# Third of three fused blocks: convolution stages woven into other attention pairs, norm and pointwise product moved to the third pair

## The chip, the core and the metric

The kernel runs on one core of one Trainium2 chip. The metric is the device time of one execution in microseconds. All three blocks are one program; only the order of the third block is changed, together with one engine choice and one buffer count.

## The reference, cut to what matters

S = 1024 rows, D = 1024 channels, f32. Two earlier blocks hand x to the third:

```python
def third_block(x, ln_g, w_in, b_in, dw_w, dw_b, cln_g, cln_b, pw_w, pw_b, rpb,
              gn_conv_g, gn_att_g, w_out, final_g):
...
        hn = rms_norm(h, ln_g[l])
        proj = hn @ w_in[l] + b_in[l]
        glu_a, glu_b, z_conv, q, k, v, z_att = jnp.split(proj, cuts, axis=-1)
        y_conv = conformer_conv(glu_a, glu_b, dw_w[l], dw_b[l], cln_g[l], cln_b[l],
                                pw_w[l], pw_b[l])
        y_att = neighbourhood_attention(q, k, v, rpb[l])
        y_conv = grouped_rms_norm(y_conv, gn_conv_g[l], CONV_GROUPS) * jax.nn.silu(z_conv)
        y_att = grouped_rms_norm(y_att, gn_att_g[l], N_HEADS) * jax.nn.silu(z_att)
        y = jnp.concatenate([y_conv, y_att], axis=-1)
        h = h + y @ w_out[l]
    return rms_norm(h, final_g)
```

`conformer_conv` is u = a * sigmoid(b), a depthwise convolution of 31 taps along the rows, a layer norm over 512 channels, silu, and a product with a 512 x 512 matrix. `neighbourhood_attention` has 8 heads of 64 channels; each position sees a window of the 16 x 64 grid.

## The kernel before

All arrays that products read are kept feature-major: 128 channels on the partitions, positions along the free axis, in two halves of 512 positions. A product in f32 is made of three matmuls per 128 channels (`mm3`, L95, L96, L97): high x high, high x low, low x high, each 128x128 by 128x512. `weight()` loads one 128x1024 piece of a matrix by SP's queue, casts the high part (on DVE, L86, or on ACT, L84, when the list `hi_on` holds True) and makes the low part on POOL (L87). A product of one weight over one half of x is 24 matmuls.

Each engine executes its instructions in the order in which the program was scheduled; the order in which the code is written is its input. A PSUM tile that collects a product comes from the group "mm" (two buffers) or "mf" (one buffer), chosen by `lane`. Scores have their own "sp" (two), transposes "tr" (two), attention's output "pv" (one).

Block 3 is built of generators. `glu(i)` makes channels i*128.. of u from two weights (ACT tanh, DVE L1290, L1291). `dwconv(i, u)` is 31 instructions on DVE over 128x1024 (L1302 once, L1304 thirty times) and stores the result to DRAM (cv_d). `conv_ln(hf)` takes four tiles of 128 positions: load, four transposes (L1315), norm statistics, `xn` (L784), four transposes back (L1320), scale and bias and tanh on ACT, and the split into `cn` high and low. `conv_pw(hf)` multiplies `cn` with two weights, 48 matmuls, into v, and runs a gate after each weight. `zgate(i)` is one product of w_in with x, stored to DRAM (z_d). `na_pair(hp)`, called p0 to p3 here, handles two heads: 144 matmuls of projections q, k and v, the gate of the pair before, a yield, then eight attention steps (4 per head; scores L323, L324 into sp, transposes L346, products L359 into pv, the sum to `aT` L366). `group_norm_gate` is a gate: squares, a matmul that sums them (L1251 into "mf"), a copy to `gr` (L1252), Ln and Exp on ACT, two products on DVE (L1259, L1260), one on POOL, and the store to y_d; its z and gr have one buffer each. `known()` is the output product over the first six of eight channel pieces, 288 matmuls (tiles y3a), `w_out` the step in it. After the gate of p3 come the last 96 matmuls and the final norm.

`weave(main, *streams)` advances the streams by a share of their yields after each attention step of main; a number behind a generator is its count of yields, the last number of a stream is the number of steps over which it is spread.

In the order before, convolutions 0 and 1 run beside the first products and p0's projections, 2 and 3 in p0's attention; the norm and pointwise product of half 0 are in p1, of half 1 in p2, with zgates beside them; `known()` is in p3.

Of the kernel before, what the change touches and what calls it, by code (L numbers as in the profile page):

```python
# [10 lines left out]
F32 = mybir.dt.float32  # L11
# [7 lines left out]
P = 128  # L19
S = 1024  # L20
# [11 lines left out]
def kernel(ctx: ExitStack, tc: tile.TileContext, a, out, blocks=(1, 2, 3)):  # L32
    nc = tc.nc
    mm = nc.tensor.matmul
# [13 lines left out]
    def f(ap):  # L48
        return ap.bitcast(F32)
# [49 lines left out]
    lane, turn = ["any"], [0]  # L99
# [92 lines left out]
    def weave(main, *streams):  # L192


        left = [[st[0], [g for g, _ in st[1]], 0, sum(c for _, c in st[1]) / st[2]] for st in streams]

        def steps(st, upto):
            while st[1] and (upto is None or st[2] < upto):
                with on(st[0]):
                    if next(st[1][0], None) is None:  # L200
                        st[1].pop(0)
                    else:
                        st[2] += 1

        for i, _ in enumerate(main):
            for st in left:
                steps(st, st[3] * (i + 1))
        for st in left:
            steps(st, None)
# [50 lines left out]
    def heads_k(dst, dlo, src, hf, bias=None, view=same, dup=False):  # L260
        for h in range(2):
            o = 64 * h
            b = None if bias is None else bias[o:o + 64]
            hi, sv = view(dst[o:o + 64, h], src[o:o + 64], hf)
            if b is None:
                act(out=hi, in_=sv, func=AF.Copy)
            else:
                act(out=hi, in_=sv, func=AF.Identity, bias=b)
            other = view(dst[64 - o:128 - o, h], src[o:o + 64], hf)[0]
            if dup:  # L270
                nc.scalar.copy(other, hi)
            else:
                nc.gpsimd.tensor_copy(other, hi)
            for q in range(2) if dup else (h,):
                d, _ = view(dlo[64 * q:64 * q + 64, h] if len(dlo.shape) == 3 else dlo[o:o + 64], src[o:o + 64], hf)
                if b is None:
                    tt(out=d, in0=sv, in1=f(hi), op=ALU.subtract)
                else:
                    stt(out=d, in0=sv, scalar=b, in1=f(hi), op0=ALU.add, op1=ALU.subtract)  # L279
# [988 lines left out]
    def block3(x3, begin, finish):  # L1268
        x_st, x_fm = x3
        w3 = a["w_in_3"]  # L1270
        TAP, PAD = 31, 15
# [4 lines left out]
        np_ = pool("na", side="right", c=nas)  # L1276
# [3 lines left out]
        cp = pool("conv", side="right", c=us)  # L1280

        def glu(i):
            wb, wa = weight(w3[4 + i]), weight(w3[i])
            u = cp.tile([P, S + 2 * PAD], F32, name="u", tag="u", bufs=2)
            nc.gpsimd.memset(u[:, 0:PAD], 0.0)
            nc.gpsimd.memset(u[:, S + PAD:], 0.0)
            for hf in range(2):
                sg = cp.tile([P, HS], F32, name="sg", tag="sg", bufs=1)
                act(out=sg, in_=fm(wb, x_fm[hf]), func=AF.Tanh, scale=0.5, bias=col("b_in_3", 4 + i, half))
                ts(out=sg, in0=sg, scalar1=1.0, scalar2=0.5, op0=ALU.add, op1=ALU.mult)  # L1290
                stt(out=u[:, PAD + hf * HS:PAD + (hf + 1) * HS], in0=fm(wa, x_fm[hf]), scalar=col("b_in_3", i), in1=sg,  # L1291
                    op0=ALU.add, op1=ALU.mult)
                yield 1
            return u

        def dwconv(i, u):
            y = cp.tile([P, S], F32, name="cy", tag="cy", bufs=2)
            for k in range(TAP):
                w = col("dw_w_3", 4 * k + i)
                src = u[:, k:k + S]  # L1300
                if k == 0:
                    ts(out=y, in0=src, scalar1=w, scalar2=col("dw_b_3", i), op0=ALU.mult, op1=ALU.add)  # L1302
                else:
                    stt(out=y, in0=src, scalar=w, in1=y, op0=ALU.mult, op1=ALU.add)  # L1304
            nc.sync.dma_start(cv_d[i], y)

        def conv_ln(cp2, n_fm, hf):
# [42 lines left out]
        def zgate(pl, i):  # L1350
            j = 8 + i if i < 4 else 20 + i
            wz = weight(w3[j])
            for hf in range(2):
                zr = pl.tile([P, HS], F32, name="zr", tag="zr", bufs=2)
                act(out=zr, in_=fm(wz, x_fm[hf]), func=AF.Identity, bias=col("b_in_3", j))
                nc.sync.dma_start(z_d[i, :, hf * HS:(hf + 1) * HS], zr)
                yield 1
# [3 lines left out]
        def na_pair(hp):  # L1361
            wq, wk, wv = (weight(w3[j * 4 + hp]) for j in (3, 4, 5))
            qs = np_.tile([P, 2, S], F32R, name="qs", tag="qs", bufs=1)
            ks = np_.tile([P, 2, S], F32R, name="ks", tag="ks", bufs=1)
            kl = np_.tile([P, S], F32R, name="kl", tag="kl", bufs=1)
            vs = np_.tile([P, 2, NT, P], F32R, name="vs", tag="vs", bufs=1)
            vt = np_.tile([P, S], F32, name="vt", tag="pth", bufs=1)
            for hf in range(2):
                heads_q(qs, fm(wq, x_fm[hf]), hf, col("b_in_3", 12 + hp), to_grid_rev)
            for hf in range(2):  # L1370
                heads_k(ks, kl, fm(wk, x_fm[hf]), hf, col("b_in_3", 16 + hp), to_grid)
            if pend:
                for _ in na_gate(*pend.pop()):
                    pass
            for hf in range(2):
                d, sv = to_grid(vt, fm(wv, x_fm[hf]), hf)
                act(out=d, in_=sv, func=AF.Identity, bias=col("b_in_3", 20 + hp))
            heads_v(vs, vt)
            yield "in"
            aT = np_.tile([P, S], F32, name="aT", tag="vt", bufs=1)  # L1380
            for h in range(2):
                hd = 2 * hp + h
                hk = np_.tile([P, 384], F32, name="hk", tag="hk", bufs=1)
                nc.scalar.dma_start(hk, bass.AP(tensor=rpb_d.tensor, offset=rpb_d.offset + hd * 496,
                                                ap=[[16, 8], [8 * 496, 16], [1, 384]]))
                bias = np_.tile([P, 768], F32, name="bias", tag="bias", bufs=1)
                for j in range(2):
                    sl = slice(384 * j, 384 * (j + 1))
                    stt(out=bias[:, sl], in0=hk, scalar=8.0, in1=mask[:, sl], op0=ALU.mult, op1=ALU.add)

                def bias_of(t):
                    o = 0 if t in (0, NT - 1) else 384
                    return bias[:, o + (P if t == 0 else 0):o + (256 if t == NT - 1 else 384)]

                def dst_of(u, src, aT=aT, h=h):
                    o = aT[64 * h:64 * h + 64].rearrange("p (r c) -> p c r", c=64)[:, 16 * u:16 * u + 16]
                    return o, src.rearrange("p (c r) -> p c r", r=16)

                yield from attend_steps(np_, qs[:, h], qs[64 * h:64 * h + 64, h], ks[:, h], kl[64 * h:64 * h + 64], vs[:, h],
                                        bias_of, lambda t: (max(0, t - 1), min(NT, t + 2)), dst_of, smax=384, rev=True)  # L1400
            pend.append((hp, aT))
# [7 lines left out]
                for hf in range(2):  # L1409
                    split(last[hf][0][:, 0], last[hf][1][:, 0], r[:, hf])  # L1410

        def conv_in(i):
            u = yield from glu(i)
            dwconv(i, u)

        convs = [conv_in(i) for i in range(2)]
        lane[0] = "any"
        for c_ in convs:
            next(c_)
        lane[0] = "mf"  # L1420
        for c_ in convs:
            for _ in c_:
                pass
        lane[0] = "mm"
        hi_on[0] = True
        p0 = na_pair(0)
        next(p0)
        weave(p0, ("mf", [(conv_in(2), 2), (conv_in(3), 2), (zgate(np_, 4), 2)], 7))
        us.close()
        hi_on[0] = False  # L1430
        with ExitStack() as c:
            cp2 = pool("conv2", side="right", c=c)
            n_fm = [[], []]
            p1 = na_pair(1)
            next(p1)
            weave(p1, ("mf", [(conv_ln(cp2, n_fm[0], 0), 4)], 4),
                  ("mm", [(zgate(np_, i), 2) for i in (5, 0, 1, 2, 3)] + [(conv_pw(cp2, n_fm[0], 0), 6)], 8))
            p2 = na_pair(2)
            next(p2)
            weave(p2, ("mf", [(conv_ln(cp2, n_fm[1], 1), 4)], 4),  # L1440
                  ("mm", [(zgate(np_, i), 2) for i in (6, 7)] + [(conv_pw(cp2, n_fm[1], 1), 6)], 8))
            p3 = na_pair(3)
            next(p3)
        x_st.close()

        with ExitStack() as c:
# [27 lines left out]
            g = np_.tile([P, D], F32, name="fg", tag="qs", bufs=1)  # L1474
# [143 lines left out]
```

## Time and profile before

| | |
|---|---|
| time, median of 3 runs | 3422.62 us (3420.29 to 3425.85) |
| time of the profiled execution | 3422.53 us |
| its span | 3420.8 us |
| granted PE clock, mean | 0.975 |
| PE busy | 3239.9 us, 14976 matmuls |
| DVE busy | 2073.7 us |
| POOL busy | 1383.7 us |
| ACT busy | 1059.6 us |
| block 3, within the span | about 2786 to 3421 us |

The span is the time from the first to the last instruction of the profile; 1.7 us lie around it. PE's busy share is that of matmuls in flight, and a matmul at a lower granted clock counts longer. The shares are means over blocks that run quite differently, so a stage is read from its own stretch.

### The profile page before, as it was taken

What the parts mean: (1) busy time and instruction counts of PE and PEld (TensorE: products, weight loads), DVE (VectorE), ACT (ScalarE), POOL (GpSimd) and SP (SyncE); (2) the same over time, 40 slices, a digit from 0 to 9 for tenths busy, and PEclk for the clock granted to TensorE, in tenths of its full rate; (3) what the DMA queues carried; (4) which work ended last, traced back from release to release, by engine and by line L of the source; (5) the groups of instructions that cost most, each with busy time, mean ns of one, the idle gap of its engine ahead of it and who ended that gap; (6) DMA issues with size and microseconds to landing.
All of it is one profiled execution on the core that took longest, in us unless ns stands there. A gap on an engine that the chain in (4) does not pass through costs nothing. (4 is left out here: it accounts for less than half of the span.)

```text
span 3420.8 us, 39879 instructions
## 1 busy us (share of the span) xinstructions
PE 3239.9 (95%) x14976; PEld 2655.8 (78%) x14976; DVE 2073.7 (61%) x3256; ACT 1059.6 (31%) x1998; POOL 1383.7 (40%) x913
## 2 busy tenths in 40 slices
PE   7999999999999999999978999999999988998998
PEld 6888887877888788778867777788888866776776
DVE  5455556375444455557768866545445579995665
ACT  3333311032333310321235632332231132235552
POOL 3111131266555643233434367655564362132221
PEclk9999999999999999999999999999999998998899
DMA  4211124212222422222252121222243221122241
GB/s 139 69 58 57 60 71 164 77 47 71 78 84 83 152 97 63 92 72 90 87 187 62 38 74 59 74 84 83 84 148 99 80 89 38 59 84 83 79 148 68
DMA packets 107473, 293.33 MB, mean 86 GB/s; under 512 B 15232, under 2 KB 20608, under 8 KB 107280
## 3 DMA queue, kind: packets, MB, share of 16 engines
q1 hardware_dynamic: 79184, 240.75, 21.3%
q10 hardware_dynamic: 28096, 50.04, 4.3%
q8 instruction: 118, 1.93, 0.2%
q14 instruction: 75, 0.61, 0.1%
HBM read 227.24 MB, written 63.76 MB: 85 GB/s over the span
## 5 line engine op out<-in xcount | busy, mean ns | idle before, releaser
L87 POOL TENSOR_TENSOR w_lo<-w_raw,w_hi 128x1024 fp32r<-128x1024 f32 x187 | 470.3, 2520 | 1130.6 <-DVE w_hi L86 653.5
L95 PE MATMUL mm<-x,w_hi 128*128 128x512 f32 x688 | 276.5, 402 | 13.0 <-DVE kl L279 8.0
L96 PE MATMUL mm<-x,w_hi 128*128 128x512 f32 x688 | 273.9, 398 | 0.0
L97 PE MATMUL mm<-x,w_lo 128*128 128x512 f32 x688 | 272.5, 397 | 1.1 <-POOL w_lo L87 1.1
L438 POOL TENSOR_TENSOR w_lo<-s,w_hi 128x512 fp32r<-128x512 f32 x160 | 220.7, 1387 | 104.4 <-ACT w_hi L437 104.0
L95 PE MATMUL mf<-x,w_hi 128*128 128x512 f32 x576 | 232.0, 403 | 4.6 <-DVE u L1291 1.6
L97 PE MATMUL mf<-x,w_lo 128*128 128x512 f32 x576 | 228.2, 396 | 1.2 <-POOL w_lo L87 1.2
L96 PE MATMUL mf<-x,w_hi 128*128 128x512 f32 x576 | 229.0, 398 | 0.0
L565 DVE TENSOR_TENSOR h<-h,mm 128x512 f32<-128x512 f32 x214 | 146.6, 686 | 134.7 <-PE mm L97 134.6
L86 DVE CAST w_hi<-w_raw 128x1024 fp32r<-128x1024 f32 x143 | 135.6, 949 | 128.5 <-PE mm L96 55.6
L438 POOL TENSOR_TENSOR w_lo<-w_raw,w_hi 128x512 fp32r<-128x512 f32 x120 | 171.6, 1430 | 96.8 <-ACT w_hi L437 96.6
L1304 DVE SCALAR_TENSOR_TENSOR cy<-u,cols,cy 128x1024 f32<-128x1024 f32 x120 | 180.6, 1524 | 0.9
L519 DVE TENSOR_TENSOR u<-p,pb 128x512 f32<-128x512 f32 x40 | 27.5, 687 | 249.1 <-PE pb L97 249.1
L437 ACT CAST w_hi<-s 128x512 fp32r<-128x512 f32 x160 | 97.2, 619 | 243.6 <-PE pc L96 148.2
L95 PEld LDWEIGHTS mm<-x,w_hi 128*128 128x128 f32 x688 | 130.5, 190 | 44.4 <-issue 12.1
L335 ACT ACTIVATE st<-st,nmax 128x128 f32<-128x128 f32 (+5 forms) x192 | 119.3, 623 | 116.0 <-DVE nmax L329 110.1
L95 PE MATMUL mm<-w_hi,act 128*128 128x512 f32 x384 | 150.5, 392 | 2.9 <-DVE h L565 2.9
L97 PEld LDWEIGHTS mm<-x,w_lo 128*128 128x128 f32 x688 | 130.4, 189 | 29.4 <-POOL w_lo L87 1.7
L96 PEld LDWEIGHTS mm<-x,w_hi 128*128 128x128 f32 x688 | 130.6, 190 | 26.1 <-issue 1.6
L96 PE MATMUL mm<-w_lo,act 128*128 128x512 f32 x384 | 150.5, 392 | 0.3 <-POOL w_lo L87 0.3
L97 PE MATMUL mm<-w_hi,act 128*128 128x512 f32 x384 | 150.3, 392 | 0.0
L137 ACT ACTIVATE pth<-tr 128x512 fp32r<-128x512 f32 (+3 forms) x224 | 95.8, 451 | 148.6 <-PE tr L346 108.2
(502 smaller groups left out, 8876.4 us busy)
## 6 DMA issues: line engine op xcount, KB each, us to landing
w_raw<-in_w_ffn_in_dram SPq DMA_DIRECT2D x88, 512.0 KB
w_raw<-in_w_in_dram SPq DMA_DIRECT2D x78, 512.0 KB
act_d<-ao SPq DMA_DIRECT2D x88, 256.0 KB
w_raw<-in_w_ffn_out_dram SPq DMA_DIRECT2D x44, 512.0 KB
act<-act_d SPq DMA_DIRECT2D x36, 512.0 KB
w_raw<-in_w_out_dram SPq DMA_DIRECT2D x24, 512.0 KB
gates_d<-go SPq DMA_DIRECT2D x32, 256.0 KB
gt<-gates_d ACTq DMA_DIRECT2D x32, 256.0 KB
```

The costliest lines, as they stand in the source:

```text
L86: nc.vector.tensor_copy(hi, raw)
L87: nc.gpsimd.tensor_tensor(out=lo, in0=raw, in1=f(hi), op=ALU.subtract)
L95: mm(out_, lh, rh, start=start and i == 0, stop=False, **kw)
L96: mm(out_, lh, rl, start=False, stop=False, **kw)
L97: mm(out_, ll, rh, start=False, stop=stop and i == n - 1, **kw)
L137: act(out=hi, in_=src, func=AF.Copy, scale=scale)
L335: act(out=st[:, :w + extra], in_=st[:, :w + extra], func=AF.Exp, scale=-1.0, bias=nmax, accum_out=ssum)
L437: nc.scalar.copy(hi, src)
L438: eng(out=lo, in0=src, in1=f(hi), op=ALU.subtract)
L519: tt(out=u3, in0=p1, in1=pb, op=ALU.add)
L565: tt(out=hh, in0=hh, in1=pt, op=ALU.add)
L1304: stt(out=y, in0=src, scalar=w, in1=y, op0=ALU.mult, op1=ALU.add)
```

## The change

Four things are different. In `heads_k` the second copy of k goes to ACT instead of POOL where there is a bias, which is so in block 3. u has four buffers instead of two. `dwconv` yields after each four taps. And the order of block 3 is written anew: glu 0 and then glu 1; p0's projections, convolution 0, p0's attention with glu 2 and 3, zgate 4 and convolution 1; p1's projections, convolution 2, p1's attention with the seven other zgates and convolution 3; p2's attention with norm and pointwise product of both halves, all in "mf"; p3 as before.

```diff
@@ -267,7 +267,7 @@
             else:
                 act(out=hi, in_=sv, func=AF.Identity, bias=b)
             other = view(dst[64 - o:128 - o, h], src[o:o + 64], hf)[0]
-            if dup:
+            if dup or b is not None:
                 nc.scalar.copy(other, hi)
             else:
                 nc.gpsimd.tensor_copy(other, hi)
@@ -1281,7 +1281,7 @@
 
         def glu(i):
             wb, wa = weight(w3[4 + i]), weight(w3[i])
-            u = cp.tile([P, S + 2 * PAD], F32, name="u", tag="u", bufs=2)
+            u = cp.tile([P, S + 2 * PAD], F32, name="u", tag="u", bufs=4)
             nc.gpsimd.memset(u[:, 0:PAD], 0.0)
             nc.gpsimd.memset(u[:, S + PAD:], 0.0)
             for hf in range(2):
@@ -1302,6 +1302,8 @@
                     ts(out=y, in0=src, scalar1=w, scalar2=col("dw_b_3", i), op0=ALU.mult, op1=ALU.add)
                 else:
                     stt(out=y, in0=src, scalar=w, in1=y, op0=ALU.mult, op1=ALU.add)
+                if k % 4 == 3:
+                    yield 1
             nc.sync.dma_start(cv_d[i], y)
 
         def conv_ln(cp2, n_fm, hf):
@@ -1409,36 +1411,37 @@
                 for hf in range(2):
                     split(last[hf][0][:, 0], last[hf][1][:, 0], r[:, hf])
 
-        def conv_in(i):
-            u = yield from glu(i)
-            dwconv(i, u)
-
-        convs = [conv_in(i) for i in range(2)]
+        us_ = {}
+
+        def glu_in(i):
+            us_[i] = yield from glu(i)
+
+        def run(gen):
+            for _ in gen:
+                pass
+
         lane[0] = "any"
-        for c_ in convs:
-            next(c_)
-        lane[0] = "mf"
-        for c_ in convs:
-            for _ in c_:
-                pass
+        run(glu_in(0))
+        run(glu_in(1))
         lane[0] = "mm"
         hi_on[0] = True
         p0 = na_pair(0)
         next(p0)
-        weave(p0, ("mf", [(conv_in(2), 2), (conv_in(3), 2), (zgate(np_, 4), 2)], 7))
+        run(dwconv(0, us_[0]))
+        weave(p0, ("mf", [(glu_in(2), 2), (glu_in(3), 2), (zgate(np_, 4), 2)], 7), ("mm", [(dwconv(1, us_[1]), 8)], 8))
+        p1 = na_pair(1)
+        next(p1)
+        run(dwconv(2, us_[2]))
+        weave(p1, ("mf", [(zgate(np_, i), 2) for i in (5, 0, 1, 2, 3, 6, 7)], 8), ("mm", [(dwconv(3, us_[3]), 8)], 8))
         us.close()
         hi_on[0] = False
         with ExitStack() as c:
             cp2 = pool("conv2", side="right", c=c)
             n_fm = [[], []]
-            p1 = na_pair(1)
-            next(p1)
-            weave(p1, ("mf", [(conv_ln(cp2, n_fm[0], 0), 4)], 4),
-                  ("mm", [(zgate(np_, i), 2) for i in (5, 0, 1, 2, 3)] + [(conv_pw(cp2, n_fm[0], 0), 6)], 8))
             p2 = na_pair(2)
             next(p2)
-            weave(p2, ("mf", [(conv_ln(cp2, n_fm[1], 1), 4)], 4),
-                  ("mm", [(zgate(np_, i), 2) for i in (6, 7)] + [(conv_pw(cp2, n_fm[1], 1), 6)], 8))
+            weave(p2, ("mf", [g for hf in range(2) for g in ((conv_ln(cp2, n_fm[hf], hf), 4),
+                                                             (conv_pw(cp2, n_fm[hf], hf), 6))], 8))
             p3 = na_pair(3)
             next(p3)
         x_st.close()
```

How the order of instructions moves, at three places. The first is DVE at the start of the convolutions; x with a number is a tile of the input in feature-major form, cut into high and low parts from the transposes tr. Before:

```order
L139 TENSOR_TENSOR x_20918<-tr,x_20916 128x4x128
L1290 TENSOR_SCALAR sg<-sg 128x512
L139 TENSOR_TENSOR x_20917<-tr,x_20915 128x4x128
L1291 SCALAR_TENSOR_TENSOR u<-mf,cols,sg 128x512
L139 TENSOR_TENSOR x_20918<-tr,x_20916 128x4x128
L1290 TENSOR_SCALAR sg<-sg 128x512
L1291 SCALAR_TENSOR_TENSOR u<-mf,cols,sg 128x512
L1302 TENSOR_SCALAR cy<-u,cols 128x1024
L1304 SCALAR_TENSOR_TENSOR cy<-u,cols,cy 128x1024 x3
```

Of the change, at the same place:

```order
L139 TENSOR_TENSOR x_20918<-tr,x_20916 128x4x128
L139 TENSOR_TENSOR x_20917<-tr,x_20915 128x4x128
L139 TENSOR_TENSOR x_20918<-tr,x_20916 128x4x128
L1391 SCALAR_TENSOR_TENSOR bias<-hk,mask 128x384 x2
L1290 TENSOR_SCALAR sg<-sg 128x512
L1291 SCALAR_TENSOR_TENSOR u<-mm,cols,sg 128x512
L1290 TENSOR_SCALAR sg<-sg 128x512
L1291 SCALAR_TENSOR_TENSOR u<-mf,cols,sg 128x512
L1302 TENSOR_SCALAR cy<-u,cols 128x1024
L1304 SCALAR_TENSOR_TENSOR cy<-u,cols,cy 128x1024 x4
```

The last splits of x (L139) now stand together ahead of the GLU's operations instead of between them.

The second place is PE in the attention of p2: sp are scores, tr transposes of the probabilities, mm and mf products. Before:

```order
L323 MATMUL sp<-ks,qs 128x384
L346 MATMUL tr<-sq_c,st 128x128 x3
L324 MATMUL sp<-kl,qs 128x384
L323 MATMUL sp<-ks,qs 128x384
L324 MATMUL sp<-kl,qs 128x384
L346 MATMUL tr<-sq_c,st 128x128 x3
L95 MATMUL mm<-x_20915,w_hi 128x512
L96 MATMUL mm<-x_20917,w_hi 128x512
L97 MATMUL mm<-x_20915,w_lo 128x512
L95 MATMUL mm<-x_20915,w_hi 128x512
L96 MATMUL mm<-x_20917,w_hi 128x512
L97 MATMUL mm<-x_20915,w_lo 128x512
```

Of the change, in p2's attention (L1317 and L1322 are the norm's two groups of transposes, L1315 and L1320 before):

```order
L359 MATMUL pv<-ptl,vs 128x256 x2
L1317 MATMUL mf<-sq_c,cv 128x128 x4
L323 MATMUL sp<-ks,qs 128x384
L324 MATMUL sp<-kl,qs 128x384
L346 MATMUL tr<-sq_c,st 128x128 x2
L359 MATMUL pv<-pth,vs 128x256
L359 MATMUL pv<-pth,vs 128x128
L359 MATMUL pv<-ptl,vs 128x128
L359 MATMUL pv<-pth,vs 128x256
L323 MATMUL sp<-ks,qs 128x384
L324 MATMUL sp<-kl,qs 128x384
```

The products with x stand no longer between the steps; they have gone to p1's attention and in front of p2's.

The third place is PE after the last projection matmul of p3 (the L95 to L97 with x in the rows before). Before:

```order
L95 MATMUL mm<-x_20916,w_hi 128x512
L96 MATMUL mm<-x_20918,w_hi 128x512
L97 MATMUL mm<-x_20916,w_lo 128x512
L323 MATMUL sp<-ks,qs 128x256
L324 MATMUL sp<-kl,qs 128x256
L323 MATMUL sp<-ks,qs 128x384
L324 MATMUL sp<-kl,qs 128x384
L293 MATMUL tr<-sq_c,vt 128x128 x8
L323 MATMUL sp<-ks,qs 128x384
L324 MATMUL sp<-kl,qs 128x384
L323 MATMUL sp<-ks,qs 128x384
L324 MATMUL sp<-kl,qs 128x384
```

Of the change, the end of the piece that stands between the projections and the first w_out (cn is the normed convolution, y3a the gated output that w_out reads):

```order
L95 MATMUL mf<-cn_24497,w_hi 128x512
L96 MATMUL mf<-cn_24498,w_hi 128x512
L97 MATMUL mf<-cn_24497,w_lo 128x512
L1251 MATMUL mf<-sq,sq_c 128x512 x6
L359 MATMUL pv<-pth,vs 128x256
L359 MATMUL pv<-pth,vs 128x128
L359 MATMUL pv<-ptl,vs 128x128
L359 MATMUL pv<-pth,vs 128x128
L359 MATMUL pv<-ptl,vs 128x128
L359 MATMUL pv<-pth,vs 128x256
L359 MATMUL pv<-ptl,vs 128x256 x2
L95 MATMUL mm<-w_hi,y3a 128x512
```

Before, the first w_out matmul (L95 on y3a) stands directly behind the rows shown; now the product on cn and six sums of squares (L1251) stand in front of it, and of the pv of attention's second step.

## Rows read from the trace of the kernel before

**Rows 1.** Part 1 of the page: busy time, share of the span, instructions

```profile
PE 3239.9 (95%) x14976; PEld 2655.8 (78%) x14976; DVE 2073.7 (61%) x3256; ACT 1059.6 (31%) x1998; POOL 1383.7 (40%) x913
```

**Rows 2.** Stretches: length, busy us of PE, PEld, DVE, ACT, POOL; PE clock

```profile
2824.00:3078.00 254.00, 229.30 (x991) 180.56 (x990) 251.67 (x308) 70.58 (x138) 64.02 (x30) 0.93 0.18 60
3171.00:3231.00 60.00, 56.02 (x252) 43.42 (x250) 43.45 (x112) 33.36 (x83) 12.51 (x8) 0.82 0.22 74
3247.00:3292.00 45.00, 42.82 (x179) 31.95 (x178) 23.68 (x37) 29.62 (x37) 17.64 (x11) 1.00 0.34 114
3292.00:3380.00 88.00, 85.67 (x402) 66.79 (x400) 52.66 (x119) 27.69 (x71) 9.88 (x4) 1.00 0.28 104
```

**Rows 3.** DVE, start of the convolutions: start us, us, operation [idle before <-releaser]

```profile
2798.71 1.27 DVE L172 SCALAR_TENSOR_TENSOR xn<-h,rstd,g 128x1024 f32<-128x1024 f32 x1
2810.14 0.68 DVE L139 TENSOR_TENSOR x<-tr,x 128x512 fp32r<-128x512 f32 x1
2824.43 0.81 DVE L1302 TENSOR_SCALAR cy<-u,cols 128x1024 f32<-128x1024 f32 x1
```

**Rows 4.** DVE groups, 2824 to 3078: busy us, mean ns | idle before

```profile
L1304 DVE SCALAR_TENSOR_TENSOR cy<-u,cols,cy 128x1024 f32<-128x1024 f32 x120 | 180.6, 1524 | 0.9
L329 DVE CUSTOM_DVE_ANT_0 st<-sp,bias 128x384 f32<-128x384 f32 (+1 forms) x24 | 11.9, 512 | 0.1
L139 DVE TENSOR_TENSOR ptl<-tr,pth 128x384 fp32r<-128x384 f32 (+1 forms) x24 | 11.8, 511 | 0.0
L341 DVE TENSOR_SCALAR st<-st,ssum 128x384 f32<-128x384 f32 (+1 forms) x24 | 10.9, 478 | 0.0
L86 DVE CAST w_hi<-w_raw 128x1024 fp32r<-128x1024 f32 x10 | 7.0, 703 | 0.6 <-PE mf L96 0.5
L366 DVE TENSOR_TENSOR aT<-pv,part 64x256 f32<-64x256 f32 x11 | 6.6, 602 | 0.1
```

**Rows 5.** DVE and POOL from 2860 us, beside one convolution

```profile
2860.94 2.46 DVE L1304 SCALAR_TENSOR_TENSOR cy<-u,cols,cy 128x1024 f32<-128x1024 f32 x2
2861.79 2.08 POOL L273 CAST ks<-ks 64x512 fp32r<-64x512 f32 x1 [8.80 <-ACT ks L268]
2863.96 2.37 POOL L87 TENSOR_TENSOR w_lo<-w_raw,w_hi 128x1024 fp32r<-128x1024 f32 x1
2864.22 3.19 DVE L1304 SCALAR_TENSOR_TENSOR cy<-u,cols,cy 128x1024 f32<-128x1024 f32 x1
```

**Rows 6.** PE: end of the third pair's projections, 21 matmuls, first score

```profile
3166.41 0.39 PE L95 MATMUL mm<-x,w_hi 128*128 128x512 f32 x1
3171.20 0.28 PE L323 MATMUL sp<-ks,qs 128*128 128x256 f32 x1
```

**Rows 7.** PE: products pv of two steps of the third pair's attention

```profile
3212.59 0.69 PE L359 MATMUL pv<-pth,vs 128*128 128x256 f32 x2
3230.88 0.55 PE L359 MATMUL pv<-pth,vs 128*128 128x256 f32 x1 [1.68 <-ACT cn L137]
```

**Rows 8.** PE: conv_ln's second transposes of tiles 0 and 3, half 0

```profile
3090.17 0.66 PE L1320 MATMUL mf<-sq_c,xn 128*128 128x128 f32 x4
3114.14 1.09 PE L1320 MATMUL mf<-sq_c,xn 128*128 128x128 f32 x4 [3.66 <-DVE xn L784]
```

**Rows 9.** PE and DVE: three gates, the fourth pair's first score, first w_out

```profile
3248.84 0.59 PE L1251 MATMUL mf<-sq,sq_c 128*128 128x512 f32 x1
3264.68 0.69 DVE L1252 COPY gr<-mf 128x512 f32<-128x512 f32 x1 [5.05 <-DMA y_d<-gr]
3287.65 1.42 DVE L1260 SCALAR_TENSOR_TENSOR gr<-aT,half,gr 128x512 f32<-128x512 f32 x2 [0.25 <-ACT gr L1255]
3286.92 0.28 PE L323 MATMUL sp<-ks,qs 128*128 128x256 f32 x1
3291.54 0.50 PE L95 MATMUL mm<-w_hi,y3a 128*128 128x512 f32 x1
```

**Rows 10.** PE: the last gate's square sums

```profile
3380.33 1.10 PE L1251 MATMUL mf<-sq,sq_c 128*128 128x512 f32 x2 [0.24 <-DVE gr L1252]
```

## The prediction, made before the changed kernel ran

> **What bounds the kernel now.** I read the page's busy times first: PE is busy 95% of the span [rows 1], so what counts is how long PE runs with gaps or at a lower clock. Blocks 1 and 2 keep their order, so the sum begins at 2786 us. The table of stretches then shows that block 3 is no single regime [rows 2]. From 2824 to 3078 us DVE is busy 251.67 of 254 us: the 124 convolution instructions fix this stage, and PE fills its gaps at a clock of 0.93. From 3171 to 3231 us the clock is 0.82 and PE has 252 instructions in 60 us: attention of the third pair without enough products beside it. From 3292 to 3380 us PE is busy 85.67 of 88 us at full clock: attention of the fourth pair with the 288 matmuls of `known`. Last come the groups of DVE instructions [rows 4] and a few times out of the timeline [rows 3, 5 to 10].
>
> All paces for the sum are rows. A product matmul on full-clock PE takes (3171.20 − 3166.41)/21 = 0.228 us [rows 6]. An attention step without products beside it takes (3230.88 − 3212.59)/3 = 6.1 us, three steps lying between the two rows [rows 7]. A tile of `conv_ln` comes every (3114.14 − 3090.17)/3 = 8.0 us [rows 8]. In the stretch from 3292 us, 288 × 0.228 = 65.7 us of PE's 85.67 are `known`, which leaves 20 us for eight attention steps: 2.5 us of PE for a step [rows 2, 6].
>
> **The change part by part.** *An earlier start of the convolutions.* The first convolution starts at 2824.43 us, since `glu(0)` and `glu(1)` share their halves and the last split of x ends at 2810.14 + 0.68 [rows 3]. In the new order glu 0 is written whole before glu 1, and the last transposes of x stand together: after the last xn ends at 2798.71 + 1.27 = 2800 us I give them 2.5 us, then come the 48 matmuls of half 1 (10.9 us by the pace) and about 0.7 us for u. So 2814 instead of 2824.4: 10.5 us gained. At worst nothing is gained; at best all of the 14 us after the last split, less 11.
>
> *DVE is relieved in the convolution stage.* Between the first and the last convolution instruction the order loses ten casts of weights (`hi_on` stays True through p1, so ACT casts), two attention tiles' worth of L329, L139, L341, two L366; a few bias and GLU operations leave and come, which I let cancel. From the groups: 7.0 + 2 × (0.51 + 0.51 + 0.48) + 2 × 0.6 = 11.2 us [rows 4]. DVE never idles there, so the stage shrinks by as much: 242 instead of 253 us, ending at 2814 + 242 = 3056. ACT, which takes over casts and copies, is busy only 70.58 of 254 us [rows 2], so nothing is queued behind them that DVE lacks.
>
> *The eight copies ks that move from POOL to ACT.* I put them at 0: POOL is busy 64 of 254 us [rows 2], and two convolution instructions beside a copy took 2.46 us, 1.23 each, no more than is seen elsewhere; it was the copy that stretched to 2.08 us. Beside the two-input w_lo a convolution instruction took 3.19 us [rows 5]. The other bound: all contention vanishes, 120 × (1.524 − 1.23) = 35 us [rows 4, 5]. But w_lo stays where it is, so I take the end near 0. The Trainium skill, "SBUF — State Buffer", section "Who interferes with whom", says that DVE and GpSimd share one port pair as an exclusive lock. By that rule eight copies of 1.5 us off POOL would give some 12 us more, and a time near 3455; the pair at 2.46 us speaks against it for this copy, the 3.19 us beside w_lo for it.
>
> *The rest of p1, and p2's projections.* When the convolutions end, five of p1's eight steps remain, each with 24 product matmuls: 24 × 0.228 + about 2 = 7.5 us, so 37 us. Behind them stand p2's projections and the last zgate halves, 236 matmuls, 54 us, and about 1 us of evictions. So p2's attention starts at 3056 + 37 + 55 = 3148 instead of 3171.2: the new order is 23 us ahead.
>
> *p2's attention has lost its products.* Before, zgates 6 and 7 and the pointwise product of half 0 stood between its scores; now only `conv_ln`'s transposes do, as the order shows. Eight steps at 7.0 us (bounds 6.1, bare [rows 7], and 8.0, the cadence of a norm tile [rows 8]): 56 us, to 3204. Then 191 matmuls of the first pointwise product and p3's projections, 43.5 us, and 7 us for the gates among them, whose copies to `gr` wait for the y_d store as seen in the old place (5.05 us idle [rows 9]): p3's projections end at 3254.5; before, p3's first score stood at 3286.92, 4.6 us ahead of the first w_out [rows 9]. Now 32 us ahead.
>
> *What the new order puts behind that: norm, product, three gates in series.* All of `conv_ln` half 1, the 48 matmuls on cn and six L1251 stand on PE's queue after the last projection matmul and ahead of the second step's pv of p3 and the first w_out. Everything with product matmuls to give is behind them in PE's queue; only a few scores and transposes of p3 stand between. Norm: four tiles at 8.0 plus 5 for the last tile's evictions and split = 37 us (bounds 24, at 6.1 a step, and 39). Product: 48 × 0.228 = 10.9 at full clock, doubled at the lower clock, one buffer of mf only: 14 (bounds 11 and 22). Gates: before, the same three run from 3248.84 to 3287.65 + 1.42, 40 us, stretched by single z and gr buffers and by the y_d store [rows 9]: 40 (bounds 34 and 43). Together 91: the first w_out at 3345.5 instead of 3291.5, 54 us late. That these 45 us of old gates cost nothing before is because PE was busy 42.82 of 45 us beside them, with projections [rows 2]; that cover now stands earlier.
>
> *The rest.* From first w_out to the last gate's squares it was 3380.33 − 3291.54 = 88.8 us [rows 9, 10]. The scores of three steps are already done, so 65.7 + 14 = 80 (bounds 75 and 88.8): 3425.5. The last 96 matmuls and the final norm are the same 40.5 us to the end: 3466.
>
> Sum against the profiled execution: span 3420.8 − 10.5 − 11 (conv) − 1.5 (p1, p2's projections) − 9 (p2's attention and p3's projections) + 86 (91 us instead of 4.6) − 9 (rest) = 3466. With the 1.7 us around the span, **3467 us**; the profiled execution stands at 3422.5, the median at 3422.6, so nothing is to be corrected.
>
> **The rivals.** *The serial stretch is short (not slower).* If norm, product and gates take 46 us and not 91, the time comes to 3422 and the early gain pays for all. This needs the tiles of half 1 to be normed already during p2's attention or p3's projections, so that after the last projection matmul only the product and the gates are left. For it: DVE has free time there (23.68 of 45 us [rows 2]). Against it: PE's queue keeps the order, and the transposes of half 1 are written behind p3's projections. It decides at 46 us: product 11 plus gates 35. Time 3420.
>
> *Bare service times.* Tiles at 6.1, product at 11, gates at 34 give 24 + 11 + 34 = 69 in place of 91 and so 3445. Likelier with the attention steps hidden in the norm's waits; still slower.
>
> *The convolutions are not helped.* If the start stays at 2824 or DVE is held up by the shared traffic, the 21 us are missing: 3488.
>
> *DVE loses its contention.* 35 us less in the convolution stage: 3432, still slower. *The change does nothing* would need all these orders to be unlike what runs; the engines execute in order, so I drop it.
>
> **How the numbers follow.** A run of this kernel spreads over 5.6 us, so about 0.2% (6.8 us) can be told from no change. The chances: forecast with its own bounds (3445 to 3485) 0.55, bare service times 0.15, convolutions not helped 0.07, contention gone 0.05: all slower, 0.82. The short stretch alone centres on no change, 0.08 for the same, and 0.10 for faster, when the short stretch meets a gain in the convolution stage. The range, 3418 to 3490, reaches from the short stretch to the unhelped convolutions. The likeliest case's own range is 3445 to 3485, from the ends of the serial terms (69 to 104).
>
> **What the profile after would show.** The first L1302 near 2814 and the last L1304 near 3056, DVE still without gaps between. Ten casts L86 fewer there, on ACT L84 in their place. p2's first score near 3148, a granted clock well below 0.9 in the 56 us behind it. Then, from about 3255 to 3345, a stretch with PE mostly idle, L95 on cn waiting for ACT or DVE, and L1251 waiting for the copy of the gate before; the first L95 on y3a near 3345. The forecast is wrong if that stretch holds PE busy for more than half, if the first L95 on y3a comes before 3300, or if the convolutions end later than 3075.

## The result, and the profile after

The changed kernel takes 3483.04 us (median of 4 runs, 3480.66 to 3488.13) against 3421.84 us: a ratio of 1.0179, 95% interval 1.0161 to 1.0197. It is 61 us slower. The profiled execution is the slowest of the four, 3488.13 us with a span of 3486.4, so times read from its trace add up to some 5 us more than the median.

First the same lines of the page as before: busy times, and the two lines of the 40 slices for PE and its clock, in the kernel before and then in the change.

```profile
PE   7999999999999999999978999999999988998998
PEclk9999999999999999999999999999999998998899
...
PE 3260.5 (94%) x14976; PEld 2663.9 (76%) x14976; DVE 2047.4 (59%) x3246; ACT 1080.3 (31%) x2024; POOL 1364.3 (39%) x897
...
PE   7999999999999999999979898999999899799768
...
PEclk9999999999999999999999999999999999897779
```

PE has as many instructions as before and 20 us more busy time, though its share fell [rows 1]: matmuls at a lower clock count longer. The loss stands in the slices near the end, where the clock is at 7 tenths for three slices and PE at 9, 7 and 6; before, it is at 8, 8 and 9, and PE at 8, 9 and 9. The table of stretches of block 3 says where (length, then busy us of PE, PEld, DVE, ACT, POOL with counts, PE clock):

```profile
2816.00:3056.00 240.00, 208.91 (x871) 161.34 (x870) 234.35 (x283) 75.56 (x138) 41.17 (x16) 0.91 0.17 54
3056.00:3166.00 110.00, 110.00 (x514) 89.96 (x513) 31.15 (x79) 33.75 (x69) 19.18 (x8) 1.00 0.26 85
3166.00:3225.00 59.00, 50.76 (x194) 37.14 (x194) 44.10 (x124) 39.36 (x92) 8.06 (x6) 0.65 0.14 43
3225.00:3271.00 46.00, 44.97 (x188) 34.51 (x186) 15.62 (x28) 20.47 (x31) 12.31 (x5) 1.00 0.25 81
3271.00:3311.00 40.00, 22.47 (x79) 15.31 (x78) 24.72 (x62) 23.00 (x49) 7.51 (x6) 0.56 0.18 53
3311.00:3329.00 18.00, 14.89 (x49) 10.31 (x49) 1.51 (x3) 3.38 (x5) 3.00 (x2) 0.85 0.09 29
3329.00:3368.00 39.00, 12.08 (x21) 4.35 (x20) 14.75 (x21) 21.34 (x24) 9.02 (x4) 0.56 0.32 109
3368.00:3441.00 73.00, 71.19 (x330) 57.44 (x329) 36.22 (x79) 20.05 (x48) 8.43 (x4) 0.98 0.32 115
3441.00:3487.00 46.00, 34.06 (x142) 25.83 (x140) 30.07 (x45) 16.96 (x25) 6.81 (x9) 0.96 0.23 92
```

Against the stretches of before [rows 2] three things are to be seen. The convolution stage is 240 instead of 254 us, with 871 instead of 991 instructions of PE. Then PE is busy for 110 of 110 us, at full clock. And from 3271 to 3368 us there is a stretch without a counterpart: 97 us in which PE is busy for 49, at clocks of 0.56, 0.85 and 0.56. The timeline of PE through it, with the idle time before an instruction and its releaser in brackets:

```profile
3165.79 0.28 PE L323 MATMUL sp<-ks,qs 128*128 128x256 f32 x1
...
3270.26 0.39 PE L97 MATMUL mm<-x,w_lo 128*128 128x512 f32 x1
...
3271.87 0.66 PE L1317 MATMUL mf<-sq_c,cv 128*128 128x128 f32 x4
...
3285.44 0.63 PE L359 MATMUL pv<-ptl,vs 128*128 128x256 f32 x2
...
3305.72 1.09 PE L1322 MATMUL mf<-sq_c,xn 128*128 128x128 f32 x4 [3.31 <-DVE xn L784]
...
3310.45 0.79 PE L95 MATMUL mf<-cn,w_hi 128*128 128x512 f32 x1 [3.65 <-ACT cn L137]
...
3328.54 1.12 PE L1251 MATMUL mf<-sq,sq_c 128*128 128x512 f32 x2 [0.78 <-ACT v L1342]
...
3338.24 2.07 PE L1251 MATMUL mf<-sq,sq_c 128*128 128x512 f32 x2 [6.59 <-ACT sq L1249]
...
3347.10 2.04 PE L1251 MATMUL mf<-sq,sq_c 128*128 128x512 f32 x2 [6.79 <-DVE gr L1252]
...
3365.96 0.69 PE L359 MATMUL pv<-pth,vs 128*128 128x256 f32 x2 [8.14 <-DVE aT L366]
...
3367.83 0.63 PE L95 MATMUL mm<-w_hi,y3a 128*128 128x512 f32 x1
```

p2's first score stands at 3165.79 (3171.20 before), the last projection matmul of p3 at 3270.26, and from there to the first w_out no products stand but the 48 matmuls on cn; the rest is the norm's transposes, the gates' sums, and scores, transposes and two steps' pv of p3. The norm lasts to 3310.45, with PE waiting 3 to 4 us for DVE's xn at three of the four tiles and 3.65 us for ACT's cn; the product to 3328.54; the gates to 3365.96, with waits of 6.59, 6.79 and 8.14 us. The first w_out comes at 3367.83; in the rows of before it followed p3's first score by 4.6 us [rows 9].

The last wait, 8.14 us for L366, shows how the gates come to hold PE. The first step's pv was done at 3285.44 + 0.63, yet DVE adds it into `aT` only at 3365.32:

```profile
3363.87 1.42 DVE L1260 SCALAR_TENSOR_TENSOR gr<-aT,half,gr 128x512 f32<-128x512 f32 x2 [0.26 <-ACT gr L1255]
3365.32 0.59 DVE L366 TENSOR_TENSOR aT<-pv,part 64x256 f32<-64x256 f32 x1
```

`aT` has one buffer in this kernel, and the last of the three gates is that of p2, whose products L1260 read p2's `aT`. L366 writes p3's and so comes behind them; pv has one buffer too, and the second step's pv stands ahead of the first w_out on PE. A second buffer of `aT` was not tried.

### The profile page after: what moved, and what is told of

Read it like the earlier page. It is cut to its first block, busy times and chain, and to the rows that moved or that the text cites. A ratio compares the mean times of both kernels' runs of the same rounds, so it can differ in the third digit from the quotient of the medians.

```text
span 3486.4 us, 39839 instructions
## 1 busy us (share of the span) xinstructions
PE 3260.5 (94%) x14976; PEld 2663.9 (76%) x14976; DVE 2047.4 (59%) x3246; ACT 1080.3 (31%) x2024; POOL 1364.3 (39%) x897
## 5 line engine op out<-in xcount | busy, mean ns | idle before, releaser
L95 PE MATMUL mf<-x,w_hi 128*128 128x512 f32 x664 | 269.2, 405 | 10.1 <-DVE u L1291 6.9
L97 PE MATMUL mf<-x,w_lo 128*128 128x512 f32 x664 | 264.8, 399 | 1.2 <-POOL w_lo L87 1.2
L96 PE MATMUL mf<-x,w_hi 128*128 128x512 f32 x664 | 265.3, 400 | 0.0
L95 PE MATMUL mm<-x,w_hi 128*128 128x512 f32 x600 | 240.5, 401 | 6.0 <-DVE kl L279 2.6
L96 PE MATMUL mm<-x,w_hi 128*128 128x512 f32 x600 | 239.5, 399 | 0.0
L97 PE MATMUL mm<-x,w_lo 128*128 128x512 f32 x600 | 236.9, 396 | 0.0
L1304 DVE SCALAR_TENSOR_TENSOR cy<-u,cols,cy 128x1024 f32<-128x1024 f32 x120 | 170.3, 1440 | 1.1
L95 PEld LDWEIGHTS mf<-x,w_hi 128*128 128x128 f32 x664 | 127.6, 192 | 38.9 <-DVE u L1291 7.8
L95 PE MATMUL mm<-w_hi,act 128*128 128x512 f32 x384 | 150.5, 392 | 2.9 <-DVE h L565 2.9
L97 PE MATMUL mm<-w_hi,act 128*128 128x512 f32 x384 | 150.3, 392 | 0.0
L97 PEld LDWEIGHTS mf<-x,w_lo 128*128 128x128 f32 x664 | 127.4, 192 | 27.9 <-POOL w_lo L87 1.4
L96 PEld LDWEIGHTS mf<-x,w_hi 128*128 128x128 f32 x664 | 127.4, 192 | 23.5
L95 PEld LDWEIGHTS mm<-x,w_hi 128*128 128x128 f32 x600 | 114.4, 191 | 32.2 <-issue 3.9
```

The lines of the kernel that those rows point to most:

```text
L95: mm(out_, lh, rh, start=start and i == 0, stop=False, **kw)
L96: mm(out_, lh, rl, start=False, stop=False, **kw)
L97: mm(out_, ll, rh, start=False, stop=stop and i == n - 1, **kw)
```

## The experiments

Times are compared through the ratio to the kernel before, run on the same chip. "e1" to "e11" are the labels of the runs.

**e1, the copies of k on ACT alone.** The kernel before with

```diff
-            if dup:
+            if dup or b is not None:
```

> The kernel before with one edit: the second copy of k goes to ACT in block 3. Theory of the prediction (the copy does not hold DVE up): within 3 us of before. Rival (the shared port of DVE and POOL is freed by it): 8 to 12 us faster, the convolution stage shorter by as much.

3424.2 us, ratio 1.0006 (0.9997 to 1.0015), and the last convolution instruction ends 3.6 us earlier than before in the profiled run, of which 1.2 us were there at the first. The interval leaves at most 1 us of gain. The stage is 2.4 us shorter, so the copies were a small load on it. The time alone could not tell: the next run shows that a much larger lead at this place does not reach the end.

**e2, the start alone.** The kernel before with glu 0 written whole ahead of glu 1:

```diff
-            u = cp.tile([P, S + 2 * PAD], F32, name="u", tag="u", bufs=2)
+            u = cp.tile([P, S + 2 * PAD], F32, name="u", tag="u", bufs=4)
...
         for c_ in convs:
-            next(c_)
-        lane[0] = "mf"
-        for c_ in convs:
             for _ in c_:
                 pass
```

> The kernel before with the start of the convolutions alone: glu 0 whole, then glu 1, four buffers for u. The first L1302 near 2815 instead of 2824. Theory: the lead of about 9 us lasts to the end, 3412 us. Rival (the stretch behind the convolutions is bound by PE, and the products pushed out of the convolution stage eat the lead): within 3 us of before, p2's first score near 3171.

3422.25 us, ratio 0.9998 (0.9989 to 1.0007): the rival. The first L1302 does stand at 2814.58 and the last L1304 ends at 3059.6, 17.7 us ahead, yet p2's transposes of v come only 2.4 us earlier (3174.66 against 3177.07). The table of stretches of this kernel, the convolution stage and what follows to p2's scores:

```profile
2814.00:3059.00 245.00, 219.16 (x936) 171.05 (x935) 240.14 (x288) 65.40 (x126) 63.76 (x25) 0.92 0.17 56
3059.00:3168.00 109.00, 100.94 (x445) 77.78 (x444) 56.22 (x123) 56.43 (x104) 27.45 (x17) 0.94 0.31 101
```

The stage is shorter, but PE has got 936 instructions done in it instead of 991 [rows 2]. What it did not do, it has to do behind it: 319 product matmuls stand between the last convolution instruction and p2's transposes of v, and 249 before. At 0.228 us each the 70 more are 16 us, about what is lost of the lead.

**e3, the whole front, with the pairs as before.** The change's front; convolutions 2 and 3 are written in p0, and p1 and p2 are those of the kernel before:

```diff
-        weave(p0, (... (zgate(np_, 4), 2)], 7), ("mm", [(dwconv(1, us_[1]), 8)], 8))
-        p1 = na_pair(1)
...
+        weave(p0, (... (zgate(np_, 4), 2)], 7),
+              ("mm", [(dwconv(1, us_[1]), 8), (later(2), 8), (later(3), 8)], 8))
         us.close()
```

> The changed kernel's front (start, weaving of the convolutions, four buffers, copies of k on ACT) with all convolutions written in the first pair, and the second and third pair as before: norm and product of half 0 in the second, of half 1 in the third. Theory of the prediction: the front is a gain of 15 to 20 us, about 3403 us. Rival (the front itself costs, or gains nothing): 3420 us or more.

3418.52 us, ratio 0.9990 (0.9980 to 1.0000): 3 to 4 us at the most likely and 7 at most, not 15 to 20. The front costs nothing, and gives little.

**e4, the back alone.** The front of before, then the second and third pair of the change:

```diff
+        p1 = na_pair(1)
+        next(p1)
+        weave(p1, ("mf", [(zgate(np_, i), 2) for i in (5, 0, 1, 2, 3, 6, 7)], 8))
         us.close()
...
+            weave(p2, ("mf", [g for hf in range(2) for g in ((conv_ln(cp2, n_fm[hf], hf), 4),
+                                                             (conv_pw(cp2, n_fm[hf], hf), 6))], 8))
```

> The front of the kernel before, and the second and third pair of the change: all zgates in the second, norm and product of both halves in the third, in mf. Theory: the chain of norm, product and three gates behind the fourth pair's projections is there again, 90 to 100 us between last projection matmul and first w_out, and the time is 3490 to 3500 us. Rival (the loss of the change comes from its front): under 3440 us.

3485.45 us, ratio 1.0183 (1.0169 to 1.0198): as slow as the whole change, and 5 us below the range that I expected. The last projection matmul of p3 and the first w_out in PE's timeline:

```profile
3265.48 0.39 PE L97 MATMUL mm<-x,w_lo 128*128 128x512 f32 x1
...
3364.28 0.63 PE L95 MATMUL mm<-w_hi,y3a 128*128 128x512 f32 x1
```

The 99 us between them are there with the old front too. This shows that the loss belongs to the new order of the second and third pair; the intervals leave the front at most some 7 us of it.

**e5, two buffers of gr in the gates.**

```diff
-        r = pl.tile([P, 2, HS], F32, name="gr", tag="gr", bufs=1)
+        r = pl.tile([P, 2, HS], F32, name="gr", tag="gr", bufs=2)
```

> The change with two buffers of gr, so that a gate's copy does not wait for the store of the gate before. Theory: the gates are a chain of ACT, DVE, POOL and a store in which this store is one link; in the change's trace two copies waited 7.2 us at most for it, so 7 to 14 us faster than the change, 3470 to 3476. Rival (the gates are held by ACT's tables and POOL alone): within 3 us of the change, 3480 to 3486.

3485.95 us, ratio 1.0185 (1.0170 to 1.0200) against the change's 1.0179: no gain to be seen, though the two intervals leave room for one of up to 6 us. In the change's trace a copy does wait for the store of the gate before:

```profile
3346.26 0.69 DVE L1252 COPY gr<-mf 128x512 f32<-128x512 f32 x1 [7.16 <-DMA y_d<-gr]
```

With two buffers the stretch from the first square sum to the first w_out is 35.4 instead of 39.3 us, by these two rows of PE in e5:

```profile
3332.22 1.12 PE L1251 MATMUL mf<-sq,sq_c 128*128 128x512 f32 x2 [0.78 <-ACT v L1342]
...
3367.59 0.80 PE L95 MATMUL mm<-w_hi,y3a 128*128 128x512 f32 x1 [3.03 <-ACT y3a L1151]
```

The first w_out comes no earlier for it (3367.83 in the change), since the first square sum comes 3.7 us later; 2.8 us of that stand already at the first convolution instruction, 2818.26 against 2815.45, ahead of the edited gates. The price that I put on the store, 7 to 14 us, was too high.

**e6, the change without the gates of half 1's product.**

```diff
+                if hf:
+                    for j, v in enumerate(vs):
+                        nc.sync.dma_start(y_d[i + j, :, c], v)
+                    continue
                 late = group_norm_gate(cp2, vs, ...
```

> The change without the two gates of the pointwise product of half 1: their squares, norm and multiplication by z are left out, and v is stored as it is. Theory: two of the three gates in series are gone from the stretch in which PE has nothing else, 25 to 30 us faster than the change, 3453 to 3458. Rival (something else holds the first w_out, the gates only lie beside it): within 5 us of the change.

3457.18 us, ratio 1.0101 (1.0084 to 1.0118), which is 26 us less than the change: what was expected. In PE's timeline the last gate's second square sum and the first w_out:

```profile
3328.79 1.10 PE L1251 MATMUL mf<-sq,sq_c 128*128 128x512 f32 x2 [0.88 <-DVE gr L1252]
...
3331.81 0.80 PE L95 MATMUL mm<-w_hi,y3a 128*128 128x512 f32 x1 [1.93 <-ACT y3a L1151]
```

The first w_out comes 36 us earlier than in the change. Of these, 10 are given back: from it to the end of the span are 128.6 us (3331.81 to 3460.4) instead of 118.6. More of p3's attention stands behind it, 50 pv matmuls (L359) instead of 42; whether that is all of the 10 us is not shown.

**e7, the products in mm.** The change with each step of `conv_pw` in the lane of two buffers:

```diff
-                                                             (conv_pw(cp2, n_fm[hf], hf), 6))], 8))
+                                                             (in_lane("mm", conv_pw(cp2, n_fm[hf], hf)), 6))], 8))
```

> The change with the pointwise products in mm instead of mf, the norm in mf as before. In PE's order the norm and product of half 1 come ahead of the fourth pair's projections, and the gates stand among the projections. Theory: the gates (39 us) are covered by projections again, the norm of half 1 still stands bare; about 40 us faster than the change, 3440 to 3450. Rival (the order of the pairs itself is the loss, whichever buffers): within 10 us of the change.

3465.38 us, ratio 1.0127 (1.0112 to 1.0142): 18 us faster than the change, half of what I expected. The table of stretches of this kernel, norm of half 1, then p3's projections with the gates, then `known`:

```profile
3248.00:3284.00 36.00, 10.76 (x34) 6.10 (x34) 14.71 (x28) 16.78 (x30) 5.36 (x5) 0.50 0.14 44
3284.00:3341.00 57.00, 55.34 (x220) 41.76 (x220) 24.21 (x41) 34.83 (x48) 15.19 (x7) 0.96 0.26 90
3341.00:3426.00 85.00, 82.95 (x394) 65.67 (x395) 50.30 (x115) 26.41 (x68) 12.03 (x5) 1.00 0.31 114
```

The norm now stands ahead of the projections and is bare (10.76 of 36 us busy, clock 0.50). The gates lie beside the projections, PE busy 55.34 of 57 us: they are hidden, and the first w_out comes at 3341.73 instead of 3367.83. Of these 26 us, 9 are given back behind it, 127.4 us to the end instead of 118.6, as in e6.

**e8, the same with zgates 6 and 7 in the third pair.**

```diff
-        weave(p1, ("mf", [(zgate(np_, i), 2) for i in (5, 0, 1, 2, 3, 6, 7)], 8), ...
+        weave(p1, ("mf", [(zgate(np_, i), 2) for i in (5, 0, 1, 2, 3)], 8), ...
...
+                  ("mm", [(zgate(np_, i), 2) for i in (6, 7)], 8))
```

> As the one with products in mm, with zgates 6 and 7 moved from the second pair to the third, in mm. Theory: 96 matmuls (22 us of PE) come from a stretch in which PE is busy to one with gaps, 5 to 20 us faster than the same without them. Rival (the scheduled order puts them where PE is busy anyway): no difference to it.

3464.04 us, ratio 1.0125 (1.0110 to 1.0140): no difference to e7 that can be seen; the intervals leave room for some 7 us. The norm of half 1 stays as bare as it was (tiles at 3240.61 to 3261.85, 7.1 us each); the 96 matmuls are gone from the stretch ahead of p2's attention (its transposes of v at 3146.51, in e7 at 3168.31), and more than half of that lead is lost again by the first w_out (3331.61, in e7 at 3341.73). Of the 6.8 us that are left between the two traces at the end the medians show 1.3, since the profiled run of e7 is 5.5 us above its median.

**e9 and e10, 27 of the 31 taps**, in the kernel before and in the change:

```diff
+        TAPS = 27
...
-            for k in range(TAP):
+            for k in range(TAPS):
```

> The kernel before with 27 of the 31 taps (four taps of each convolution are left out): 16 convolution instructions less on DVE, some 20 to 24 us of its time in the stage that DVE fills. Theory formed from the runs with the new start and the new front: PE has to do the products that this stage then no longer covers, so the gain is under 8 us. Rival (the stage is DVE's and its end is the program's lead, as the prediction's sum took it): 18 us or more faster than before, 3400 to 3404.

3411.58 us, ratio 0.9968 (0.9956 to 0.9981): 11 us, between both expectations. The last convolution instruction ends 25.5 us earlier, p2's transposes of v come 11.2 us earlier (3165.92). So in the kernel before somewhat less than half of what DVE saves gets through. Most of the rest is counted in the two traces: 306 product matmuls instead of 249 stand between the last convolution instruction and p2's transposes of v, and the 57 more are 13 us.

> The change with the same 27 of 31 taps. Theory: PE is busy without gaps from the end of the convolutions to the third pair's scores, so under 8 us faster than the change, 3475 to 3483. Rival: 18 us or more, 3460 to 3465.

3481.41 us, ratio 1.0168 (1.0155 to 1.0182): 4 us less than the change by the ratios, with intervals that overlap. Its convolutions end 18.8 us earlier, p2's transposes of v come 10.7 us earlier (3157.37 against 3168.02), p3's last projection matmul 4.0 us (3266.30). So the size is as expected but the reason only in part: the stretch of PE behind the convolutions takes 8 of the 19 us (20 product matmuls more, 432 instead of 412, are 4.6 of them), and the third pair takes 7 of the 11 that are left. Why it does, with the same 192 product matmuls, is not shown.

**e11, the new front, the product of half 0 behind the third pair's projections.** As e3, with

```diff
-                  ("mm", [(zgate(np_, i), 2) for i in (5, 0, 1, 2, 3)] + [(conv_pw(cp2, n_fm[0], 0), 6)], 8))
+                  ("mm", [(zgate(np_, i), 2) for i in (5, 0, 1, 2, 3)], 8))
             p2 = na_pair(2)
             next(p2)
+            run(conv_pw(cp2, n_fm[0], 0))
```

> The new front with the old pairs, and the product and gates of half 0 written behind the third pair's projections instead of within the second pair. Theory (what counts is whether PE has products beside each chain of norm and attention): the projections fill the norm of half 0, the products of half 0 come beside the third pair's attention; 5 to 15 us faster than the new front alone, 3403 to 3413. Rival (those gaps come back in the third pair, where the norm of half 1 is then later): within 4 us of 3418.

3415.94 us, ratio 0.9977 (0.9967 to 0.9986): 8 us faster than the kernel before and the fastest that computes everything, but only some 4 us faster than e3 by the two ratios, whose intervals overlap; that is the rival's side. The stretch with the norm of half 0 in e3, and the third pair behind it:

```profile
3060.00:3148.00 88.00, 82.16 (x374) 63.99 (x373) 45.70 (x109) 42.48 (x88) 18.64 (x11) 0.92 0.30 94
3148.00:3240.00 92.00, 85.78 (x385) 66.49 (x384) 56.40 (x138) 53.75 (x112) 19.39 (x12) 0.89 0.23 80
```

and in e11, the same two stretches:

```profile
3060.00:3148.00 88.00, 88.00 (x428) 70.54 (x426) 52.01 (x122) 44.85 (x96) 15.46 (x11) 1.00 0.26 83
3148.00:3240.00 92.00, 79.44 (x344) 60.45 (x344) 51.66 (x127) 52.00 (x106) 23.34 (x13) 0.85 0.28 90
```

PE is now busy for 88 of 88 us at full clock, and has done 428 instead of 374 instructions. The gaps have moved on: 79.44 of 92 us at 0.85 in the third pair, where e3 has 85.78 at 0.89.

## Why the prediction was right, step by step

The sign, the size (3467 forecast, 3483 measured, inside the range) and the mechanism of the loss hold. Two terms were mis-sized: the lead at p2's first score was put 18 us too high and the serial stretch 7 us too low, and the reason behind the first failed. With the lead as it came out the same sum gives 3485. That 3483 lies inside even the likeliest case's own range, 3445 to 3485, owes something to luck: that range allowed for the serial terms alone, and most of the miss came from the lead.

*The start and the end of the convolutions* came as forecast, 2814 and 3056. The third row is the group of the 120 instructions between them, with busy us and mean ns:

```profile
2815.45 2.69 DVE L1302 TENSOR_SCALAR cy<-u,cols 128x1024 f32<-128x1024 f32 x1
...
3052.99 2.60 DVE L1304 SCALAR_TENSOR_TENSOR cy<-u,cols,cy 128x1024 f32<-128x1024 f32 x2
...
L1304 DVE SCALAR_TENSOR_TENSOR cy<-u,cols,cy 128x1024 f32<-128x1024 f32 x120 | 170.3, 1440 | 1.1
```

The sum is better than its parts. DVE's busy time in the stage fell by 17 us (251.67 to 234.35), not by 11, since the convolution instructions themselves took 10 us less, 1440 ns each instead of 1524 [rows 4], where I had left contention as it was. Against that DVE had gaps of 5.7 us, where I had forecast none. With only the copies of k gone the mean is 1509 ns (e1); what brought the rest is not separated.

*"p2's attention starts at 3056 + 37 + 55 = 3148"* is the term that failed in size: it started at 3165.79. I counted 24 matmuls for each of five steps and 236 behind them, 356 in all; the trace has 412 product matmuls between the last convolution instruction and p2's first score, and 56 × 0.228 = 13 us of the 18 are these. What stands behind it is a step of mine that was wrong in kind: that the end of DVE's stage is the program's lead. e2 and e3 show it, and e9 and e10 show that only part of a larger saving gets through. The prediction itself says that PE fills its gaps beside the convolutions; I did not then ask what happens to those products when the stage gets shorter. PE's busy time from 2786 us to p2's first scores is 346 us before (265.46 + 80.65) and 346 us after (236.36 + 110.00), by these stretches of before and then of the change:

```profile
2786.00:3078.00 292.00, 265.46 (x1161) 209.94 (x1161) 270.73 (x331) 80.39 (x152) 76.42 (x38) 0.94 0.19 63
3078.00:3171.00 93.00, 80.65 (x342) 61.99 (x341) 48.87 (x102) 51.22 (x92) 24.78 (x16) 0.87 0.29 96
...
2786.00:3056.00 270.00, 236.36 (x992) 183.26 (x992) 250.11 (x304) 85.08 (x152) 53.39 (x32) 0.91 0.18 57
3056.00:3166.00 110.00, 110.00 (x514) 89.96 (x513) 31.15 (x79) 33.75 (x69) 19.18 (x8) 1.00 0.26 85
```

*p2's attention and p3's projections*, 106.5 us forecast, took 104.5, with a clock of 0.65 in the attention.

*The serial stretch*, 91 us forecast, took 97.6 from the last projection matmul: to the product 40.2 (37 forecast), the product 18.1 (14), the gates 39.3 (40). The norm's tiles came 8.9 us apart in the mean, not 8.0. Of the product the first 12 matmuls ran at the lower clock, one each 0.43 us (1.2 GHz), and only the rest near 0.23 us (2.4 GHz); with one buffer of mf PE also waited 0.78 us for ACT's v behind each 12. e4 shows the whole loss with this stretch in it and the old front. e6 shows that the gates are on the path in it: without two of them the first w_out comes 36 us earlier, as it does by 26 where they are covered (e7). At the end of the program 26 and 18 us of that are left. That the norm is on the path too is read from the timelines of the change and of e7; no run takes it away.

*The rest and the end* came as forecast. The point that the forecast took is the second square sum of the last gate, 3380.33 before and 3446.98 now: 79.2 us from the first w_out (80 forecast) and 39.4 us from there to the end (40.5). The last gate's first square sum stands 6.1 us ahead of it in the new order, with w_out matmuls of other tiles between them, and before 2.0 us (3378.37).

```profile
3440.86 1.02 PE L1251 MATMUL mf<-sq,sq_c 128*128 128x512 f32 x2
...
3446.98 1.02 PE L1251 MATMUL mf<-sq,sq_c 128*128 128x512 f32 x2
```

Of the rivals, the short stretch (46 us) and the bare service times (69 us) are refuted by the trace, which has 97.6. Of the 35 us of DVE's contention some 10 did go, within the stage of the convolutions. The unhelped convolutions (3488) come near the time for another reason: the convolutions were helped, and only 5 us of that were left at p2's first score. The copies on ACT are worth nothing at the end, as forecast (e1), and 2.4 us in the stage. The 12 us that I estimated from the rule of the Trainium skill, "SBUF — State Buffer", section "Who interferes with whom", are not there, but that does not speak against the rule: the 1.5 us that I took for a copy held a wait of the copy's own. Nor did the pair at 2.46 us speak against it, as I had read it: there it was the copy that waited. The rows for both stand below, and they agree with the rule.

## What to carry to other kernels

A chain of small steps (norm, product, gates) cost next to nothing here as long as products stood in the same stretch of PE's queue (the old gates: PE busy 42.82 of 45 us), and most of its length where the order let them pass it (97.6 us bare, 61 lost). So count for each chain which products are still there to stand beside it, not how much work is left in all. And a shorter stage of another engine is not yet a lead when PE did its filling there: count the products that PE then no longer does beside it, and take their time off the lead. In e2 these were 16 us against a lead of 17.7, in e9 13 against 25.5.

## What the runs showed of the hardware that was not expected

In the change the first instruction of the first convolution took 2.69 us, though the same instruction took 0.81 us before [rows 3]. POOL's w_lo stood beside it, over the same stretch:

```profile
2815.21 2.39 POOL L87 TENSOR_TENSOR w_lo<-w_raw,w_hi 128x1024 fp32r<-128x1024 f32 x1 [1.01 <-ACT w_hi L84]
```

It ended 0.5 us behind POOL's instruction, and the one with two tensor inputs, at 3.19 us, 1.1 us behind [rows 5]: as if each had stood still until POOL was nearly done.

Beside a copy of k it is mostly the copy that stands still. In the kernel before one copy with no DVE instruction beside it took 0.61 us; the one beside the pair of convolution instructions took 2.08 us, and the pair was not held up [rows 5]. A convolution instruction that started while a copy (2866.39, 1.49 us) was running took 1.62 us, some 0.35 us more than most:

```profile
3164.30 0.61 POOL L273 CAST ks<-ks 64x512 fp32r<-64x512 f32 x1
...
2867.33 1.62 DVE L1304 SCALAR_TENSOR_TENSOR cy<-u,cols,cy 128x1024 f32<-128x1024 f32 x1
```

So my estimate for the eight copies from these rows is 8 × 0.61 = 4.9 us of DVE at most, not 12; e1 measured 2.4 us in the stage.

Where PE stands in gaps its own steps cost double too: a square sum (two records, x2 in the rows) took 1.02 us at 3440.86, in a stretch at a granted clock of 0.98, and 2.04 us at 3347.10, in the stretch at 0.56.
